# A new order for the opening of a hybrid diffusion backbone: modulation loads first, norm sums and evacuations earlier, small S5 work later

## The chip, the cores and the metric

The kernel runs on one core of a Trainium2 chip. The core has a matrix engine (TensorE, here PE, with its weight loads listed apart as PEld), a vector engine (VectorE, DVE), a scalar engine with function tables (ScalarE, ACT), a general engine (GpSimd, POOL) and a queue for loads and stores (SyncE, SP). The metric is the time of one execution on the device in microseconds, lower is better, given as a median of several runs.

## The reference

The model is a backbone of two layers over 1024 latent tokens with 256 context tokens ahead of them (1280 columns in all), 1024 channels. Both layers begin with an adaptive norm, whose shift, scale and gate come from the conditioning:

```python
def rmsnorm(x, g):
    y = xf * lax.rsqrt(jnp.mean(xf * xf, axis=-1, keepdims=True) + NORM_EPS)
def modulation(cond, w, b):
    return jnp.split(jax.nn.silu(cond) @ w + b, 3, axis=-1)
...
n_lat = rmsnorm(x, norm_g[l]) * (1.0 + sc_l[:, None]) + sh_l[:, None]
n_ctx = rmsnorm(ctx_s, norm_g[l]) * (1.0 + sc_c) + sh_c
```

Layer 0 multiplies the normed tokens with `ev_w_in` (1024 x 3072) and feeds two branches. One is a bidirectional gated recurrence (RG-LRU) behind a short convolution over time. The other is a bidirectional S5 recurrence, whose complex coefficients need sines and cosines of angles:

```python
mag = jnp.exp(lam_re * dt)
ab_re = mag * jnp.cos(lam_im * dt)
ab_im = mag * jnp.sin(lam_im * dt)
f_re = (nr * lam_re + ab_im * lam_im) / den
f_im = (ab_im * lam_re - nr * lam_im) / den
bb_re = f_re[..., None] * b_re - f_im[..., None] * b_im
```

Layer 1 is latent attention with 8 heads; a last norm follows. Everything is float32.

## The kernel before

The channels lie on the partitions and the 1280 tokens in the columns, so the input is eight tiles `xT` of 128 x 1280. A product of float32 precision is made of three passes on PE: each operand is split into a coarse part (`hi`, a cast on ACT) and the rest (`lo`, a difference on DVE), and `mm3` (L209 to L211) adds hi x hi, hi x lo and lo x hi. `split` (L182, L184) does that for weights.

All that the change touches is in `start` (L542), in helpers that it calls, and in the S5 preparation. `start` stands in a `manual_schedule` block: the instructions of each engine run in the order in which the code writes them down, and an engine that waits holds up all that is written behind it on that engine. Loads are issued in written order on SP, of which 8 are in flight; one load waits for the buffer that it overwrites. `big` is a pool of 11 slots and `far` one of 16, each slot 128 x 1280; `mw` tiles (modulation weights) have 6 buffers, `wraw` one.

The opening runs through these stages:

- **Constants and loads.** `load_const` loads small constants, `set_const` makes others, among them `cs` (the SiLU of the conditioning, L245) and `gneg` (the negated gains). `s5_turns` (L359) is a generator that works out the powers of the S5 coefficients: its first piece ends with two sines on ACT (L387, L388), the second multiplies them into powers on DVE and stores them to DRAM as `s5pow` (L390 to L397), the third has 13 small operations on 128 x 32 (L400 to L413) that give the factors `s5f`.
- **Modulation.** `mod_load` loads four `mw` tiles for one unit of 4 channel blocks; `mod_steps` multiplies them (8 matmuls, L277), copies the bank to `row` on DVE (L279), turns it by four small products (L283) and adds the bias on DVE (L287). `norm_scale` (L296) makes the scale. A unit is named (part, half): parts 0, 1, 2 are shift, scale, gate.
- **The first pair.** `pair` (L572) is a generator of ten steps that multiplies two blocks of weights with the eight channel blocks: step i does block i of the first weights (banks "mm") and block i - 2 of the second (banks "g"). `next(run)` writes one step down. The steps use x times the scale, which `x_parts` makes without waiting for the norm: split on ACT (L589) and DVE (L590), a square on ACT (L593), and a running sum `acc` on DVE (L595). Between steps stand the second scale unit (1,1) and the shift units (0,0) and (0,1).
- **The norm.** `sum_of` (L704) sums `acc` over channels on PE with a matrix of ones, in three blocks of columns of 512, 512 and 256. `neg_rstd` (L302 to L309) makes the reciprocal root of each block, with logarithm, exponential and square on ACT and two passes on DVE. `chunks` (L620) copies the finished banks away; for the second block of weights it multiplies by the norm at once, for the first the norm comes later. `shparts` are casts of the shift, two columns of which go into each `xhi` and `xlo` (L723).
- **The second and third pair**, with `normed` and `n_parts` (the normed blocks and their split), `shift_of`, `bias_of` and `put` (the bias of the first two outputs, and their store), and the gate units.
- **Angle pieces and the heads' evacuation.** Beside the third pair, `s5_phases` (L440) makes four pieces: three DVE passes over 128 x 1280 (from L447), then an absolute value and three sines on ACT (L451 to L454). `s5_small` reads the stored powers back and makes the S5 input factors. `conv_in` (L862, L863) empties a finished bank of a recurrence head: a copy and a scaled copy per block of columns on ACT; `conv_tap` (L870) adds the other three taps of the convolution on DVE, and `conv_parts` splits the result. After that the S5 weights begin (`s5_weights`, first at L480). The first SiLU evacuation of the next product on ACT is at L1093.

## Time and profile before

| | |
|---|---|
| median of 3 runs | 1595.79 us (1595.71 to 1597.96) |
| profiled execution | 1596.53 us, of which 1594.4 us from the first to the last instruction |
| mean granted clock of PE | 0.971 |
| PE, DVE, ACT busy | 94%, 71%, 52% of the span |
| bytes moved by DMA | 207.76 MB |

The profile is of one execution. Engines work side by side; what ends a stretch is the engine on which the others wait last there. Idle time of a row is given in square brackets, with the instruction that ended it. The granted clock is a share of the full 2.4 GHz.

### The profile page before, as it was taken

How to read it: one execution, taken by the hardware profiler on the slowest of the kernel's cores; microseconds unless marked ns; L12 is line 12 of the kernel's file. 1: busy time of each engine (PE TensorE's matmuls, PEld its weight loads, DVE VectorE, ACT ScalarE, POOL GpSimd, SP SyncE). 2: the span in 40 equal slices, each digit the busy share in tenths (PEclk: the TensorE clock that was granted, in tenths of full speed). 3: DMA queues.
4: the chain of work that ended last, by engine and by line, in shares of the span. 5: the costliest groups of instructions: out<-in, count | busy, mean ns of one | idle time of the engine just before them, and what ended most of it. 6: DMA issues, size and time to landing. Idle time of an engine off the chain costs nothing.

```text
span 1594.4 us, 22595 instructions
## 1 busy us (share of the span) xinstructions
PE 1495.9 (94%) x8690; PEld 1287.3 (81%) x8690; DVE 1139.5 (71%) x1858; ACT 826.0 (52%) x1422; POOL 46.5 (3%) x107
## 2 busy tenths in 40 slices
PE   6997889989998997899999999999999999999997
PEld 3675777877777876687787999878999999999887
DVE  6487779899999977622235623558888888889655
ACT  5536676678666694301124423446555565566432
POOL 0002000000000000000000000010000000000000
PEclk8898899999999998899999999999999999999999
DMA  9164544536554657555442231352111120122253
GB/s 352 68 212 160 165 143 140 178 125 193 146 153 139 180 176 248 187 178 185 157 177 93 67 87 53 121 186 73 31 50 41 63 58 17 41 93 87 92 180 119
DMA packets 96154, 207.76 MB, mean 130 GB/s; under 512 B 9904, under 2 KB 42416, under 8 KB 96048
## 3 DMA queue, kind: packets, MB, share of 16 engines
q1 hardware_dynamic: 86528, 166.65, 32.0%
q0 software_dynamic: 9520, 39.69, 7.4%
q8 instruction: 68, 1.11, 0.3%
q14 instruction: 38, 0.31, 0.1%
HBM read 143.03 MB, written 63.28 MB: 129 GB/s over the span
## 4 chain that ended last, share of the span: by engine, by line
PE 34%; issue 26%; DVE 12%; DMA 3%; ACT 1%; POOL 1%; SPq 0%; DVEq 0%; POOLq 0%; ACTq 0%
PE pv L1578 7%; PE pt L1565 4%; PE S L209 2%; PE S L210 2%; PE S L211 2%; PE S L1517 2%; PE S L1514 2%; PE S L1516 2%; PE S L1513 2%; PE S L1515 2%; DVE H L1018 1%; DVE u L870 1%; PE pt L210 1%; PE pt L211 1%; PE pt L209 1%
## 5 line engine op out<-in xcount | busy, mean ns | idle before, releaser
L182 ACT CAST w_hi<-wraw 128x1024 fp32r<-128x1024 f32 (+3 forms) x73 | 63.3, 867 | 188.1 <-PE mm L210 132.0
L209 PE MATMUL mm<-n0hi,w_hi 128*128 128x512 f32 (+1 forms) x432 | 157.7, 365 | 0.0
L210 PE MATMUL mm<-n0lo,w_hi 128*128 128x512 f32 (+1 forms) x432 | 154.9, 358 | 0.0
L211 PE MATMUL mm<-n0hi,w_lo 128*128 128x512 f32 (+1 forms) x432 | 154.1, 357 | 0.0
L1569 ACT CAST ph<-pt 128x512 fp32r<-128x512 f32 x160 | 90.9, 589 | 83.3 <-PE pt L1565 83.0
L1572 DVE TENSOR_TENSOR pl<-pt,ph 128x512 fp32r<-128x512 f32 x160 | 109.5, 686 | 19.6 <-ACT ph L1569 17.7
L209 PE MATMUL mm<-hi,w_hi 128*128 128x512 f32 (+1 forms) x264 | 101.1, 383 | 12.7 <-ACT w_hi L182 10.4
L209 PE MATMUL mm<-n1hi,w_hi 128*128 128x342 f32 (+2 forms) x336 | 109.6, 329 | 1.7 <-DVE pr L1321 1.7
L210 PE MATMUL mm<-n1lo,w_hi 128*128 128x342 f32 (+2 forms) x336 | 110.7, 329 | 0.0
L211 PE MATMUL mm<-n1hi,w_lo 128*128 128x342 f32 (+2 forms) x336 | 110.2, 328 | 0.0
L1578 PE MATMUL pv<-ph,v 128*128 128x256 f32 x640 | 107.4, 298 | 0.0
L211 PE MATMUL mm<-hi,w_lo 128*128 128x512 f32 (+1 forms) x264 | 99.7, 381 | 4.8 <-DVE w_lo L184 4.8
L210 PE MATMUL mm<-lo,w_hi 128*128 128x512 f32 (+1 forms) x264 | 99.5, 377 | 0.0
L184 DVE TENSOR_TENSOR w_lo<-wraw,w_hi 128x1024 fp32r<-128x1024 f32 (+3 forms) x73 | 72.4, 992 | 30.4 <-ACT w_hi L182 28.6
L209 PEld LDWEIGHTS mm<-n0hi,w_hi 128*128 128x128 f32 x432 | 82.4, 191 | 12.8
L211 PEld LDWEIGHTS mm<-n0hi,w_lo 128*128 128x128 f32 x432 | 81.9, 190 | 13.0
L210 PEld LDWEIGHTS mm<-n0lo,w_hi 128*128 128x128 f32 x432 | 82.1, 190 | 12.3
L1565 PE MATMUL pt<-c_ident,P 128*128 128x128 f32 x640 | 90.9, 272 | 0.6 <-DVE kl L1495 0.6
L1550 ACT ACTIVATE P<-S,sm 128x512 f32<-128x512 f32 x128 | 86.6, 688 | 0.0
L1578 PEld LDWEIGHTS pv<-ph,v 128*128 128x128 f32 x640 | 84.2, 190 | 0.2
L1565 PEld LDWEIGHTS pt<-c_ident,P 128*128 128x128 f32 x640 | 75.7, 141 | 10.5 <-DVE kl L1495 0.8
L1542 DVE TENSOR_REDUCE sm<-S 128x1 f32<-128x512 f32 x128 | 82.1, 681 | 0.7 <-PE S L1517 0.6
(420 smaller groups left out, 4031.0 us busy)
## 6 DMA issues: line engine op xcount, KB each, us to landing
mw<-in_mod_w SPq DMA_DIRECT2D x48, 512.0 KB
wraw<-in_w_in SPq DMA_DIRECT2D x24, 512.0 KB
mixdr<-r POOLq DMA_DIRECT2D x14, 640.0 KB, 5.8
s5wt<-s5scr SPq DMA_DIRECT2D x16, 512.0 KB
ph<-phdr SPq DMA_DIRECT2D x16, 480.0 KB
wraw<-in_mla_in SPq DMA_DIRECT2D x14, 512.0 KB
wraw<-in_w_out SPq DMA_DIRECT2D x16, 384.0 KB
xT<-in_xT SPq DMA_DIRECT2D x8, 640.0 KB
```

The source lines that it names most:

```text
L182: nc.scalar.copy(hi, raw)
L184: nc.vector.tensor_sub(lo, raw, hi.bitcast(F32))
L209: mm(out, w[0], x[0], start=start, stop=False)
L210: mm(out, w[0], x[1], start=False, stop=False)
L211: mm(out, w[1], x[0], start=False, stop=stop)
L1513: mm(d, q[0][:, qs], k[0][:, ks], start=True, stop=False)
L1542: nc.vector.reduce_max(x.sm[e][:, n:n + 1], x.S[e][n], axis=mybir.AxisListType.X)
L1550: nc.scalar.activation(x.P[e][:, s:s + z], x.S[e][n], AF.Exp, bias=sm[:, 4:5], scale=SCALE, accum_out=sm[:, 5 + n:6 + n])
L1565: nc.tensor.transpose(pt[:, i, e], x.P[e][:, key:key + 128], self.ident)
L1569: nc.scalar.copy(x.hi[t], x.pt[t])
L1572: nc.vector.tensor_sub(x.lo[t], x.pt[t], x.hi[t].bitcast(F32))
L1578: mm(x.pv, v[:, 128 * (h % 2):128 * (h % 2) + 128], p, start=x.left == 30, stop=x.left == 1)
```

## The change

It changes the order of the opening and moves some operations from one engine to another; what is computed stays the same.

- The conditioning is loaded first, then the S5 constants, then the first four `mw` tiles; `sel`, `mod_b` and `gains` come behind these. `gneg` moves behind the first piece of `s5_turns`.
- In `s5_turns` the square and the step 1 - 2x go from DVE to ACT (one Square and one Copy with scale and bias over 128 x 608). The two remaining products and the store are written down later, behind `x_parts(5)` and a further step of the pair. The 13 small operations go to `s5_small`, where they read the powers that were loaded back.
- The shift unit (0,0) is written ahead of `x_parts(6)`, with all its steps before the next step of the pair; the unit (0,1) and the sums of the norm stand ahead of step 7 of the pair, where they stood behind it. The third sum takes a bank "mm", and its norm block stands ahead of the casts of the shift.
- Beside the third pair the first four steps write the first two angle pieces; the third and fourth stand each between `conv_in` and the end of `conv_tap` of one head. `s5_small` is written at step 4 instead of step 1.

```diff
@@ set_const
-        nc.vector.tensor_scalar(self.gneg, self.gains[:, 0:29], -1.0, None, ALU.mult)
@@ s5_turns
...
+        nc.vector.tensor_copy(self.s5_u8, v[:, :, 18])
+        nc.vector.tensor_copy(self.s5_rho, w[:, :, 18])
         nc.scalar.activation(hs, v, AF.Sin, scale=ONE_PI)
         nc.scalar.activation(sn, v, AF.Sin, scale=TWO_PI)
+        nc.scalar.activation(hs, hs, AF.Square)
+        nc.scalar.activation(hs, hs, AF.Copy, bias=1.0, scale=-2.0)
         yield
-        nc.vector.tensor_copy(self.s5_u8, v[:, :, 18])
-        nc.vector.tensor_copy(self.s5_rho, w[:, :, 18])
-        tt(hs, hs, hs, ALU.mult)
-        ts(hs, hs, -2.0, 1.0, ALU.mult, ALU.add)
         tt(hs, hs, w, ALU.mult)
         tt(sn, sn, w, ALU.mult)
         self.s5pow = self.dram.tile([2, 128, 32 * NP], F32, name="s5pow")
         for i, p in enumerate((hs, sn)):
             nc.gpsimd.dma_start(self.s5pow[i], p.rearrange("p g k -> p (g k)"))
-        yield
-        ts(nr, hs[:, :, 17], -1.0, None, ALU.add)
-        ai = sn[:, :, 17]
...
+    def s5_small(self):
...
+        nc.vector.tensor_scalar(nr, Pre[:, :, 17], -1.0, None, ALU.add)
+        ai = Pim[:, :, 17]
         tt(den, LR, LR, ALU.mult)
...
@@ start
-            self.load_const("s5p", "kpow", "cT", "sel", "mod_b", "gains")
+            self.load_const("cT", "s5p", "kpow")
+            m = [self.mod_load(unit(1, 0), mw)]
+            self.load_const("sel", "mod_b", "gains")
             self.set_const()
             turns = self.s5_turns()
             next(turns)
-            m = [self.mod_load(unit(1, 0), mw)]
+            nc.vector.tensor_scalar(self.gneg, self.gains[:, 0:29], -1.0, None, ALU.mult)
...
             x_parts(2)
-            next(turns)
             x_parts(3)
-            next(turns, None)
             steps = self.mod_steps(unit(1, 1), m[1], self.row)
...
             x_parts(5)
             next(run)
+            next(turns, None)
             w2 = [self.split(r, mp, "wx", 2, [128, 8, 128])]
             r = raw(19)
+            steps = self.mod_steps(unit(0, 0), m[2], self.row)
+            next(steps)
             x_parts(6)
+            next(steps, None)
             x_parts(7)
-            steps = self.mod_steps(unit(0, 0), m[2], self.row)
             next(run)
+            next(run)
+            steps = self.mod_steps(unit(0, 1), m[3], self.row)
             next(steps)
-            next(run)
             next(steps, None)
...
+            sum_of(1, "s5", 2)
+            sum_of(2, "s5", 2)
+            self.neg_rstd(sums, rs, 1024)
             ps = next(run)
-            steps = self.mod_steps(unit(0, 1), m[3], self.row)
-            next(steps)
-            sum_of(1)
-            sum_of(2)
             o = [chunks(ps[0], nc.scalar.copy)]
-            self.neg_rstd(sums, rs, 1024)
+            sum_of(0, "mm", 3)
+            self.neg_rstd(sums[2:], rs, 1024)
             next(run)
-            sum_of(0)
-            next(steps, None)
...
-            self.neg_rstd(sums[2:], rs, 1024)
             ps = next(run)
...
             for i in range(10):
                 ps = next(run)
-                if i == 1:
+                if i < 4:
+                    next(phases)
+                if i == 4:
                     small = self.s5_small()
-                if i < 8:
-                    next(phases)
...
                         self.conv_in(h, p, b)
+                    next(phases)
                     for k in range(3):
                         self.conv_tap(h, k)
+                    next(phases)
```

**First place: DVE around the copy of the second scale unit.** The numbers behind the names count tiles. `row` is the copied modulation row, `s5a` the tile of the small S5 operations, `mod` the modulation. Before, DVE has in a row:

```order
L595 TENSOR_TENSOR acc_28_215<-acc_28_215,sq_291 128x1280
L400 TENSOR_SCALAR s5a_121<-s5half_128 128x32
L402 TENSOR_TENSOR s5a_121<-c_s5p 128x32
...
L409 TENSOR_TENSOR s5f<-s5a_121 128x32
...
L413 TENSOR_TENSOR s5f<-s5a_121 128x32
L279 COPY row_316<-s_49_307 128x512
L287 TENSOR_TENSOR mod_116<-s_54_339,c_mod_b 128x4 x2
```

Now DVE has:

```order
L594 TENSOR_TENSOR acc_28_218<-acc_28_218,sq_285 128x1280
L278 COPY row_297<-s_49_288 128x512
L286 TENSOR_TENSOR mod_123<-s_54_320,c_mod_b 128x4 x2
L295 SCALAR_TENSOR_TENSOR mod_123<-mod_123,gneg 128x4 x2
...
L594 TENSOR_TENSOR acc_28_218<-acc_28_218,sq_370 128x1280
L391 TENSOR_TENSOR s5half_134<-s5half_134,s5w_132 128x608
L392 TENSOR_TENSOR s5sin_133<-s5sin_133,s5w_132 128x608
L184 TENSOR_TENSOR wx_lo_398<-wraw_230,wx_hi_396 128x1024
L278 COPY row_411<-s_67_402 128x512
```

The small S5 operations are gone from between the sum `acc` and the row copy; the two S5 products and the split `wx_lo` stand between a later sum and the row copy of the next unit.

**Second place: ACT at the norm.** `chunks` is the copy of the first finished banks, `rs` the norm. Before, ACT has:

```order
L620 COPY chunks_522<-mm_237 128x8x32
L620 COPY chunks_522<-mm_238 128x8x64
L620 COPY chunks_522<-mm_239 128x8x64
L302 ACT_TABLE_LOAD
L302 ACTIVATE rs_76_488<-s_79_518,eps 128x512
L302 ACTIVATE rs_76_488<-s_80_520,eps 128x512
L306 ACT_TABLE_LOAD
L306 ACTIVATE rs_76_488<-rs_76_488 128x512
L307 ACTIVATE row_528<-rs_76_488 128x512
```

Now ACT has:

```order
L301 ACT_TABLE_LOAD
L301 ACTIVATE rs_79_492<-s_80_493,eps 128x512
L301 ACTIVATE rs_79_492<-s_81_495,eps 128x512
L305 ACT_TABLE_LOAD
L305 ACTIVATE rs_79_492<-rs_79_492 128x512
L306 ACTIVATE row_499<-rs_79_492 128x512
...
L619 COPY chunks_527<-mm_240 128x8x32
L619 COPY chunks_527<-mm_241 128x8x64
L619 COPY chunks_527<-mm_242 128x8x64
L301 ACT_TABLE_LOAD
L301 ACTIVATE rs_79_492<-mm_531,eps 128x256
```

The three copies of `chunks` stood ahead of the logarithms and stand now between the first two norm blocks and the third.

**Third place: ACT at the end of the third pair.** `cosine`, `negsin` and `phase` are the tiles of an angle piece, `wh` the coarse part of the next weights, `xa` and `u` the two copies of a head, `row_1283` and `row_1311` the SiLU evacuations of the product that follows. Before, ACT has:

```order
L451 ACTIVATE cosine_1153<-phase_1152 128x1280
...
L454 ACTIVATE cosine_1153<-cosine_1153,half_pi 128x1280
L775 CAST wh_1183<-wraw_843 128x1024
L862 COPY xa_1187<-mm_976 128x256
L863 ACTIVATE u_1188<-mm_976,c_lru 128x256
...
L862 COPY xa_1219<-g_1042 128x256
...
L1093 ACT_TABLE_LOAD
L1093 ACTIVATE row_1283<-mm_1258 128x256
```

Now ACT has:

```order
L453 ACTIVATE cosine_1019<-cosine_1019,half_pi 128x1280
L775 CAST wh_1157<-wraw_829 128x1024
L864 COPY xa_1161<-mm_962 128x256
...
L1095 ACT_TABLE_LOAD
L1095 ACTIVATE row_1283<-mm_1258 128x256
L450 ACTIVATE cosine_1170<-phase_1169 128x1280
...
L453 ACTIVATE cosine_1170<-cosine_1170,half_pi 128x1280
L864 COPY xa_1206<-g_1006 128x256
...
L1095 ACTIVATE row_1311<-mm_1286 128x512
L450 ACTIVATE cosine_1215<-phase_1214 128x1280
```

The fourth angle piece stood ahead of the weight cast and of both heads; now the second piece stands there, and the third and fourth stand behind the copies of the first and the second head, each with a SiLU evacuation ahead of it.

## Rows read from the trace of the kernel before

**Rows 1.** The page, first part: busy time, share of span, instructions.

```profile
PE 1495.9 (94%) x8690; PEld 1287.3 (81%) x8690; DVE 1139.5 (71%) x1858; ACT 826.0 (52%) x1422; POOL 46.5 (3%) x107
```

**Rows 2.** Waits of PE, 0 to 185 us: total, times, longest.

```profile
PE mm L209 <- ACT u L863: 11.2, 1, 11.2
...
PE s L283 <- DVE row L279: 6.6, 3, 4.2
```

**Rows 3.** Windows: length, PE, PEld, DVE, ACT, POOL, PEclk, DMA share, GB/s.

```profile
34.60:42.00 7.40, 7.34 (x25) 6.38 (x26) 4.64 (x10) 5.30 (x7) 0.00 (x0) 0.54 1.05 391
...
103.00:107.00 4.00, 4.00 (x14) 3.35 (x14) 4.00 (x8) 1.05 (x1) 0.00 (x0) 0.57 0.36 145
```

**Rows 4.** Timeline of the first loads and products: start, busy, engine, instruction, [idle before].

```profile
3.56 1.97 SPq L261 DMA_DIRECT2D mw<-in_mod_w  x4
...
11.87 0.69 ACT L388 ACTIVATE s5sin<-s5v 128x608 f32<-128x608 f32 x1
...
14.86 1.55 ACT L589 ACTIVATE xhi<-xT,mod 128x256 fp32r<-128x256 f32 x2 [1.09 <-DVE mod L296]
...
25.70 1.05 PE L277 MATMUL s<-mw,cs 128*32 128x512 f32 x4 [0.29 <-DMA mw<-in_mod_w]
```

**Rows 5.** Timeline of DVE, 31 to 46 us.

```profile
31.60 0.18 DVE L400 TENSOR_SCALAR s5a<-s5half 128x32 f32<-128x32 f32 x1
...
33.92 0.68 DVE L279 COPY row<-s 128x512 f32<-128x512 f32 x1
...
36.23 0.23 DVE L287 TENSOR_TENSOR mod<-s,c_mod_b 128x4 f32<-128x4 f32 x2 [1.63 <-PE s L283]
...
43.88 1.22 DVE L184 TENSOR_TENSOR wx_lo<-wraw,wx_hi 128x1024 fp32r<-128x1024 f32 x1
```

**Rows 6.** Timeline of PE, 42 to 64 us.

```profile
42.28 0.28 PE L209 MATMUL mm<-xhi,w_hi 128*128 128x256 f32 x1
...
49.42 1.92 PE L277 MATMUL s<-mw,cs 128*32 128x512 f32 x16
...
61.22 2.03 PE L704 MATMUL s<-acc,ones 128*128 128x512 f32 x4
```

**Rows 7.** Timeline of ACT and DVE at the norm, 57 to 78 us.

```profile
57.05 1.28 ACT L620 COPY chunks<-mm 128x512 f32<-128x512 f32 x2 [0.33 <-PE mm L211]
...
62.39 0.69 ACT L302 ACTIVATE rs<-s,eps 128x512 f32<-128x512 f32 x1 [2.76 <-PE s L704]
...
68.13 0.63 ACT L307 ACTIVATE row<-rs 128x512 f32<-128x512 f32 x1 [1.02 <-DVE rs L309]
...
73.65 1.28 ACT L302 ACT_TABLE_LOAD   x1
...
77.63 0.42 DVE L308 SCALAR_TENSOR_TENSOR row<-s,row 128x256 f32<-128x256 f32 x1 [5.53 <-ACT row L307]
```

**Rows 8.** Timeline of PE, start of the second pair and a gate unit.

```profile
74.61 0.42 PE L209 MATMUL mm<-xhi,wx_hi 128*128 128x258 f32 x1
...
101.90 1.05 PE L283 MATMUL s<-c_sel,row 128*128 128x2 f32 x8 [1.60 <-DVE row L279]
```

**Rows 9.** Timeline of ACT at the angle pieces, 137 to 161 us.

```profile
137.39 1.28 ACT L451 ACTIVATE cosine<-phase 128x1280 f32<-128x1280 f32 x1 [8.88 <-DVE s5bb L427]
...
145.18 1.27 ACT L451 ACTIVATE cosine<-phase 128x1280 f32<-128x1280 f32 x1 [1.37 <-DVE phase L449]
...
159.83 1.03 ACT L775 CAST wh<-wraw 128x1024 fp32r<-128x1024 f32 x1
```

**Rows 10.** Timeline of DVE, 133 to 181 us.

```profile
133.49 1.49 DVE L447 TENSOR_TENSOR phase<-s5u,c_tau 128x1280 f32<-128x1280 f32 x1
...
163.94 9.23 DVE L870 SCALAR_TENSOR_TENSOR u<-xa,c_lru,u 128x1022 f32<-128x1022 f32 x11 [1.43 <-ACT u L863]
...
180.11 0.28 DVE L480 COPY pad<-s5bb 64x256 f32<-64x256 f32 x1
```

**Rows 11.** DMA issues, 0 to 60 us: queue, count, KB each, us to landing.

```profile
s5pow<-s5sin POOLq DMA_DIRECT2D x1, 304.0 KB, 7.1
```

More of the change, by code (lines that the diff above doesn't have):

```diff
@@ L365, in s5_turns @@
         NP = 19
-        sm = self.far([128, 9, 32], name="s5a")
-        dt, lr, th, n_, u, den, nr, x1, x2 = (sm[:, i] for i in range(9))
-        self.s5_rho, self.s5_u8, self.s5_f = (c.tile([128, *z], F32, name=n)
-                                              for n, z in (("s5rho", (32,)), ("s5u8", (32,)), ("s5f", (2, 32))))
+        sm = self.far([128, 5, 32], name="s5a")
+        dt, lr, th, n_, u = (sm[:, i] for i in range(5))
+        self.s5_rho, self.s5_u8 = (c.tile([128, 32], F32, name=n) for n in ("s5rho", "s5u8"))
         v, w, sn, hs = (self.far([128, 32, NP], name=n) for n in ("s5v", "s5w", "s5sin", "s5half"))
@@ L398, in s5_turns @@
             nc.gpsimd.dma_start(self.s5pow[i], p.rearrange("p g k -> p (g k)"))
-        yield
-        ts(nr, hs[:, :, 17], -1.0, None, ALU.add)
-        ai = sn[:, :, 17]
+    def s5_small(self):
+        nc, t, sp = self.nc, self.t, self.sp
+        tt = nc.vector.tensor_tensor
+        bc = lambda a, k: a.unsqueeze(2).to_broadcast([128, 32, k])
+        Pre, Pim = (sp.tile([128, 32, 19], F32, name=n) for n in ("s5pre", "s5pim"))
+        for i, p in enumerate((Pre, Pim)):
+            nc.sync.dma_start(p.rearrange("p g k -> p (g k)"), self.s5pow[i])
+        sm = sp.tile([128, 6, 32], F32, name="s5small")
+        den, nr, fr, fi, x1, x2 = (sm[:, i] for i in range(6))
+        LR, LI = self.s5p[:, 0], self.s5p[:, 1]
+        nc.vector.tensor_scalar(nr, Pre[:, :, 17], -1.0, None, ALU.add)
+        ai = Pim[:, :, 17]
         tt(den, LR, LR, ALU.mult)
@@ L412, in s5_turns @@
         tt(x1, x1, x2, ALU.subtract)
-        tt(self.s5_f[:, 1], x1, den, ALU.mult)
-    def s5_small(self):
-        nc, t, sp = self.nc, self.t, self.sp
-        tt = nc.vector.tensor_tensor
-        bc = lambda a, k: a.unsqueeze(2).to_broadcast([128, 32, k])
-        Pre, Pim = (sp.tile([128, 32, 19], F32, name=n) for n in ("s5pre", "s5pim"))
-        for i, p in enumerate((Pre, Pim)):
-            nc.sync.dma_start(p.rearrange("p g k -> p (g k)"), self.s5pow[i])
-        fr, fi = self.s5_f[:, 0], self.s5_f[:, 1]
+        tt(fi, x1, den, ALU.mult)
         ccp = sp.tile([128, 2, 32, 16], F32, name="s5c")
```

6 lines of the change are left out of this document (3 added, 3 removed).

## The prediction

> **What bounds the kernel now.** I read the page first: TensorE (PE) is busy for 94% of the span [rows 1], so a stretch in which PE stands still is what an edit of order can win. The diff touches only the opening, the first 185 us. After it the instructions of every engine stand in the same order as before, so I ask one question: by how much earlier does the work after the opening begin? Next I read what PE waits for in 0 to 185 us [rows 2]. The longest wait is 11.2 us for ScalarE's (ACT's) `u`. The next is 6.6 us for VectorE's (DVE's) copy of the modulation row, 4.2 us of it at one place. Third, I read the clock that PE was granted [rows 3]: 0.54 in the 7.4 us after the 4.2 us wait, 0.57 in the 4.0 us that follow a wait of only 1.6 us. Those are mixtures of the levels 1.2 and 2.4 GHz, nearly all 1.2. So here a wait costs its own length and then some more in slow matmuls.
>
> I now carry the shift, new time minus old time of the same work, through the opening.
>
> **The loads.** The four `mw` loads are issued from 3.56 us [rows 4]. In the new order three small loads (`sel`, `mod_b`, `gains`) go behind them, which at about 0.45 us per issue lets the stream begin 1.4 us earlier. The first products are held by ACT instead: it gets two more passes over 608 elements (Square and Copy, which leave DVE). Nothing shows these two; the nearest row, a sine of that shape, takes 0.69 us [rows 4], so ACT is about 1.3 us longer busy. Before the first `xhi` it stood idle 1.09 us [rows 4], waiting for the modulation, so this cover and the earlier start swallow it: the first product moves by 0.9 to 1.1 us. PE then meets the second set of `mw` loads, which it already waits for at 25.70 [rows 4] and which move with the stream. Shift there: between 0 (the small loads come late, and `gneg`, now in front of the first row copy, holds DVE) and -1.4; I take **-1.2**, near the stream, since the waiting row is a load.
>
> **The S5 pieces out of DVE's way.** Before, DVE did the wide pieces ahead of the second of these two parts and the small ones from 31.60 to 33.92 [rows 5], and only then the row copy, for which PE stood 4.2 us. After, the copy stands right behind the third `acc`. DVE is there at about 28.5 us and PE comes to its small products at 29.3, so the wait is gone: -4.2. The stretch 34.6 to 42.0 at 0.54 [rows 3] holds 7.4 x 0.54 = 4.0 us of full-speed work, so without the fall of the clock -3.4. Sum at 42.0: **-8.8**; PE would stand there at 33.2 us.
>
> **A new wait.** What was moved comes back further down. The third modulation unit (`mod_steps` of unit (0,0)) is now asked for after two more pairs of products less than before, and its row copy stands on DVE behind four parts and sums, the two S5 products and the split `wx_lo`. From the second modulation on DVE (36.23 before, 30.35 now: 1.2 + 4.2 and 0.5 for slow small products) to `wx_lo` it takes 43.88 - 36.23 = 7.65 us [rows 5]. Add two S5 products at 0.69 (as wide as the sine [rows 4]), `wx_lo` itself 1.22 and the copy 0.68 [rows 5]: the copy ends at 41.3. PE needs 3.57 us for a pair of steps (42.28 to 49.42 holds two) and 1.92 for the unit [rows 6], so it is there at 39.0: a wait of **2.4 us** that did not exist. It is longer than the wait of 1.6 us after which the clock fell, so I add what 4.0 us at 0.57 lose, 1.7 us [rows 3]. PE runs on at 41.4. It then does the small products 0.9, two pairs 7.1 plus 1.7, the unit of (0,1) 1.9, the round over DVE for its row 0.9, the small products 0.8, and reaches the norm sums at 54.7. They stood at 61.22 [rows 6]. Shift **-6.5**.
>
> The part x7 now waits for the store of the S5 powers, since its tiles take their place. The store is issued at 39.2 and takes 7.1 us [rows 11], to 46.3; two passes later, at 49.3, `acc` is whole, 5 us before the sums want it. Hidden, at 0; without that cover each further microsecond of the store would be one of the sums.
>
> **The norm.** ACT's Ln follows the sums by 1.17 us (62.39 against 61.22 [rows 6, 7]), so now at 55.9. From there to the end of the second Square 68.13 + 0.63 - 62.39 = 6.4 us. Then stand the three copies of the heads' bank, which before were done while ACT waited: 1.28 for two and about 0.35 [rows 7], together 1.6, now on the path. The last norm block takes 77.63 - 73.65 = 4.0 to DVE. DVE's two passes, the two casts of the shift and the first two copies take 1.6. The second pair starts at 55.9 + 6.4 + 1.6 + 4.0 + 1.6 = 69.5; it stood at 74.61 [rows 8]. Shift **-5.1**. PE itself is done with the first pair near 68 to 69, a clock fall at the third wait (for the copy that frees the `mm` bank) included, so ACT decides.
>
> **The second and third pair.** The first products of the pair ran slow before; -0.6. At 101.90 PE waited 1.6 us for a row copy [rows 8]. DVE is now 9 us earlier and PE under 6; by the chain of shift bias, `put`, weight split and row copy the copy ends about 1 us before PE wants it. So -1.6, and -1.7 for the slow stretch behind it [rows 3]. Shift **-9.0** at the end of the third pair; the short waits at 124 us hang on PE's own work and move along.
>
> **The angle pieces.** Before, ACT did all four S5 angle pieces ahead of the heads' evacuation (`conv_in`), from 137.39 to 159.83 [rows 9], and PE stood 11.2 us. After, two stand ahead of it. With -9.0 the first DVE piece starts at 124.5 (133.49 [rows 10]) and ACT at 128.4. A first piece with its table takes 6.3, a further one (159.83 - 145.18)/3 = 4.9, the weight cast 1.0: `conv_in` starts at 140.6, the moment PE ends its third pair. So the 11.2 us are gone, and most of the slow stretch after it. But the rest is late next. DVE's line is: split 1.2, piece 3.8, six taps 6 x 9.23/11 = 5.0, piece 3.8 [rows 10], to 154.4. ACT then has a piece 4.9, a row copy 0.5 and the cast of `u` 1.2, to 161.0; DVE two differences and a split 4.05, to **165.1**, where its S5 weights begin. They began at 180.11 [rows 10]. `s5_small` gets 13 small operations, 33.92 - 31.60 = 2.3 us [rows 5]; they lie beside ACT's second piece, at 0. All queues keep their order from there. Shift **-15.0**.
>
> **Sum.** The profiled execution took 1596.53 us (span 1594.4, and 2.1 around it); 1596.53 - 15.0 = 1581.5. The median is 0.74 lower: **1580.7**.
>
> **Rivals.**
> A, *the wait at 101.90 stays*: my margin is 1 us. Then +1.6 + 1.7: 1584.0. A chance of 0.12. For: DVE is dense there. Against: it gains 4 us on PE.
> B, *the clock forgives*: no fall after the 2.4 us wait, or the norm chain runs shorter; -1.7 to -4: 1577 to 1579. 0.14.
> C, *table switches*: the row copies (SiLU) now alternate with sines on ACT. If each change loaded a table there would be four more loads at 1.28 us [rows 7], all in the chain that ends at 165.1: +5.1, 1585.8. Against: the new order shows one load, ahead of the first row copy. 0.04. The Trainium skill, "ScalarE: Activation LUTs", section "Rules for kernel authors", speaks against this interleaving: do all of one table set before switching, at some 2.7 us a switch, which would make it 1591.5. The profile has 1.28 us for a load, and no run here shows a switch at 2.7.
> D, *given back*: a later stage is paced by loads that do not move, and the time stays 1595 to 1596. For: 208 MB in all. Against: loads wait for buffers that come free earlier. 0.03.
> E, *slower, the clock stays down*: the place is the second pair, some 40 us of PE work at full clock, entered after three waits in a row (39, 53, 60 us). Each microsecond of that work done at 1.2 GHz costs one more. With 15.0 won, the kernel is slower by over 0.2% once 18 us of it run so; with half of it the time is 1600.7. Against: slow stretches lasted 4 to 7.4 us [rows 3]. 0.03.
>
> **How the numbers follow.** The forecast proper, within 2 us of 1580.7, has 0.64, A 0.12, B 0.14, C 0.04, D 0.03, E 0.03. The range takes in A, B and C with the bounds of the loads (+1.2): 1575 to 1588, and leaves about 0.1 out. A measurement can tell about 0.2%, 3.2 us, from no change. Faster by more: 0.64 + 0.12 + 0.14 + 0.04 = 0.94; within: 0.03; slower: 0.03.
>
> **What will show it.** Right: PE has no wait before the second set of small products, a new one of about 2.4 us near 39 us, sums near 54.7, the second pair near 69.5, `conv_in` near 140.6 without a PE wait of 11 us, S5 weights near 165. Wrong: a wait over 4 us at 39 us, the second pair later than 72, a table load between sine and row copy, or a stage after 185 us whose length changes by more than 2 us.

## The result, and the profile after

The changed kernel takes 1579.9 us (median of 4 runs, 1579.71 to 1580.32), beside 1596.88 us for the kernel before in the same comparison. The ratio is 0.9898 with a 95% interval of 0.9883 to 0.9913: faster by 1.0%. The forecast was 1580.7. The profiled execution took 1579.79 us, its span is 1577.7.

The first part of the page of the changed kernel (busy time, share of the span, instructions) answers to [rows 1]:

```profile
PE 1486.9 (94%) x8690; PEld 1277.5 (81%) x8690; DVE 1138.1 (72%) x1856; ACT 828.3 (52%) x1424; POOL 46.8 (3%) x107
```

The shares have hardly moved. PE is busy for 9.0 us less (1495.9 - 1486.9) with the same number of instructions, so in these two executions about that much of the 16.7 us of span is matmuls that ran at the higher clock, and the rest is idle time of PE that is gone.

What PE waits for in the first 170 us of the changed kernel (in total, times, longest), beside [rows 2]:

```profile
PE s L276 <- DMA mw<-in_mod_w: 7.2, 4, 6.4
PE g L209 <- ACT hi L1196: 4.9, 1, 4.9
PE s L282 <- DVE row L278: 2.4, 3, 0.8
...
PE mm L209 <- ACT u L865: 1.2, 1, 1.2
```

The 11.2 us for `u` are 1.2 now. The row copies cost 2.4 us in three waits of at most 0.8, which is one trip from PE to DVE and back; no copy is late any more. New is a wait of 4.9 us for `hi`, the cast of the first head's `u`.

The timeline of PE in the changed kernel at the places that the prediction named (start, busy time, instruction, idle time before):

```profile
25.14 1.05 PE L276 MATMUL s<-mw,cs 128*32 128x512 f32 x4 [0.27 <-DMA mw<-in_mod_w]
...
29.72 0.95 PE L282 MATMUL s<-c_sel,row 128*128 128x2 f32 x8
...
34.13 0.28 PE L209 MATMUL mm<-xhi,w_hi 128*128 128x256 f32 x1
...
37.73 2.22 PE L276 MATMUL s<-mw,cs 128*32 128x512 f32 x12
40.26 1.05 PE L276 MATMUL s<-mw,cs 128*32 128x512 f32 x4 [0.31 <-DMA mw<-in_mod_w]
42.11 1.05 PE L282 MATMUL s<-c_sel,row 128*128 128x2 f32 x8 [0.79 <-DVE row L278]
...
53.88 1.96 PE L707 MATMUL s<-acc,ones 128*128 128x512 f32 x4
...
66.84 0.39 PE L209 MATMUL mm<-xhi,wx_hi 128*128 128x258 f32 x1 [1.92 <-ACT xhi L724]
...
116.25 0.36 PE L209 MATMUL g<-n0hi,w_hi 128*128 128x256 f32 x1 [1.55 <-DVE chunks L621]
```

Beside [rows 4, 6, 8]: the last products of the second modulation unit, which wait for their loads in both kernels, start 0.56 us earlier (25.14 against 25.70), the step of the pair at 34.13 stood at 42.28, the norm sums begin 7.3 us earlier (53.88 against 61.22), the second pair 7.8 us (66.84 against 74.61). At 116.25 stands the first product of the third pair's second block of weights. Before, it was 8.65 us later:

```profile
124.90 0.36 PE L209 MATMUL g<-n0hi,w_hi 128*128 128x256 f32 x1 [1.50 <-DVE chunks L622]
```

ACT and DVE of the changed kernel, the last part of the input and then the evacuation:

```profile
46.57 1.55 ACT L588 ACTIVATE xhi<-xT,mod 128x256 fp32r<-128x256 f32 x2 [6.53 <-issue]
...
139.59 1.03 ACT L775 CAST wh<-wraw 128x1024 fp32r<-128x1024 f32 x1
140.53 0.36 ACT L864 COPY xa<-mm 128x256 f32<-128x256 f32 x1
...
143.69 1.28 ACT L1095 ACT_TABLE_LOAD   x1
144.99 0.39 ACT L1095 ACTIVATE row<-mm 128x256 f32<-128x256 f32 x1
145.71 1.28 ACT L450 ACTIVATE cosine<-phase 128x1280 f32<-128x1280 f32 x1 [0.34 <-DVE phase L448]
...
164.72 0.28 DVE L479 COPY pad<-s5bb 64x256 f32<-64x256 f32 x1
165.01 0.29 DVE L480 COPY pad<-s5bb 64x256 f32<-64x256 f32 x1
```

The first row is the part x7, which waits for the store of the S5 powers, forecast for 46.3. The weight cast stood at 159.83 [rows 9], 20.2 us later. `conv_in` follows at 140.53. The S5 weights start at 164.72 instead of 180.11 [rows 10]: 15.4 us earlier. Set beside each other instruction by instruction, the two traces stay 15.4 to 15.6 us apart on DVE up to 500 us and end 16.7 us apart.

### The profile page after: what moved, and what is told of

It reads as the page before. It is cut to its first block, busy times and chain, and to the rows that moved or that the text cites. A ratio compares the mean times of both kernels' runs of the same rounds, so it can differ in the third digit from the quotient of the medians.

```text
span 1577.7 us, 22599 instructions
## 1 busy us (share of the span) xinstructions
PE 1486.9 (94%) x8690; PEld 1277.5 (81%) x8690; DVE 1138.1 (72%) x1856; ACT 828.3 (52%) x1424; POOL 46.8 (3%) x107
## 4 chain that ended last, share of the span: by engine, by line
PE 35%; issue 26%; DVE 11%; DMA 2%; ACT 1%; POOL 1%; SPq 0%; DVEq 0%; POOLq 0%; ACTq 0%
PE pv L1580 7%; PE pt L1567 4%; PE S L209 2%; PE S L211 2%; PE S L210 2%; PE S L1519 2%; PE S L1518 2%; PE S L1517 2%; PE S L1516 2%; PE S L1515 2%; DVE H L1020 1%; PE mm L211 1%; PE mm L209 1%; PE mm L210 1%; PE pt L210 1%
```

## The experiments

The theory: two gains in series. The opening proper (loads, S5 work out of the way, norm order) brings the third pair forward, and the order at the evacuation brings the rest. What counts of the second is not PE's wait but where the line of DVE and ACT ends, at the S5 weights. Its rivals: PE's waits are themselves the price; one part is swallowed by the other; the clock of PE decides.

Each median below is of 4 to 6 runs. Medians of one kernel differ by up to 2 us between comparisons (the changed kernel had 1579.9 and 1577.84), so a shift of less than 2 us is read from the traces. A trace shows one execution: four executions with the same order up to the second pair (the changed kernel, `after_again`, `opening_only`, `early_hi`) have the norm sums at 53.88, 53.28, 53.29 and 54.91 us and the second pair at 66.84, 66.23, 66.25 and 67.86.

### The two parts alone

`evac_only` is the kernel before with the new loop beside the third pair; `opening_only` is the changed kernel with the old loop:

```diff
 for i in range(10):
     ps = next(run)
-    if i < 4:
-        next(phases)
-    if i == 4:
+    if i == 1:
         small = self.s5_small()
+    if i < 8:
+        next(phases)
 ...
         for b, p in enumerate(ps[h]):
             self.conv_in(h, p, b)
-        next(phases)
         for k in range(3):
             self.conv_tap(h, k)
-        next(phases)
```

That is the edit that makes `opening_only` out of the changed kernel; `evac_only` makes the reverse edit in the kernel before.

> The kernel before with the new order beside the third pair alone (two angle pieces ahead of the heads' evacuation, two between their taps). Theory 1, two gains in series with DVE's line as the limit: the third pair ends where it did, `conv_in` starts near 149.6 us (140.5 of the changed kernel and the 9.0 by which the opening is later), PE's wait of 11.2 us for `u` falls to about 1, and the S5 weights on DVE start near 173.7 us instead of 180.1, because the two late pieces then stand in DVE's and ACT's line. Time 1589.4 us, 6.4 less than before, although PE loses 10 us of waiting. Rival, PE's wait is the price: the whole 11.2 us and the slow stretch behind it are won, 1581 to 1585 us.

> The changed kernel with the old order beside the third pair (four angle pieces ahead of the evacuation, `s5_small` at step 1). Theory 1: the third pair runs 8.7 to 9.0 us earlier than before as in the changed kernel; the 13 small S5 operations, 2.3 us, now stand ahead of the second angle piece, on which ACT waits, so `conv_in` comes 6.5 us earlier than before (near 154 us) and the S5 weights near 173.5. Time 1589.3 us. Theory 1 without a price for the 13 operations: 1587.0. Rival, an earlier opening is swallowed by the angle pieces or by loads: 1594 to 1596 us.

Measured: `evac_only` 1589.66 us, ratio to the kernel before 0.9953 (0.9940 to 0.9966); `opening_only` 1586.63 us, ratio 0.9938 (0.9924 to 0.9952). The product of the two ratios is 0.9891, the whole change has 0.9898. So the parts add, and none swallows the other.

`evac_only`, timeline: ACT's first evacuation and the S5 weights on DVE:

```profile
149.61 0.37 ACT L864 COPY xa<-mm 128x256 f32<-128x256 f32 x1
...
173.79 0.28 DVE L480 COPY pad<-s5bb 64x256 f32<-64x256 f32 x1
```

The longest wait of PE behind its third pair is the one for `hi`, 4.9 us, as in the changed kernel. `conv_in` was expected at 149.6 and the S5 weights at 173.7. PE's wait of 11.2 us is gone from this kernel, yet it won 6.3 us at the S5 weights and 7.7 in time (beside 1597.38 us for the kernel before): the rest came back as the wait of 4.9 us for `hi`. The rival that prices PE's wait falls.

`opening_only`, timeline: ACT's second angle piece and first evacuation, and the S5 weights:

```profile
135.09 1.27 ACT L450 ACTIVATE cosine<-phase 128x1280 f32<-128x1280 f32 x1 [4.02 <-DVE phase L448]
...
150.66 0.36 ACT L862 COPY xa<-mm 128x256 f32<-128x256 f32 x1
...
170.92 0.28 DVE L479 COPY pad<-s5bb 64x256 f32<-64x256 f32 x1
```

Its longest wait of PE:

```profile
PE mm L209 <- ACT u L863: 15.0, 1, 15.0
```

PE has the long wait for `u` again, 15.0 us, since it comes to it earlier. ACT waits 4.02 us for the second angle piece where it waited 1.37 [rows 9]: 2.65 us more. That is the price of the 13 small operations when they stand ahead of a piece, which the prediction put at 2.3 and hid beside ACT in the changed kernel. The time is 2.7 us better than expected. In the profile the first angle piece began at 120.75 us and not at 124.49, with the same order ahead of it, which fits; but that is one execution, the fastest of the five. The section on the clock below takes it up.

### The S5 work in front of the row copy, in three doses

`s5_back` puts the four wide and the 13 small operations back on DVE ahead of the row copy of the second scale unit; `products_small_back` only the two products and the small ones; `products_back` only the two products:

```diff
             x_parts(2)
+            next(turns)
             x_parts(3)
+            next(turns, None)
...
             next(run)
-            next(turns, None)
             w2 = [self.split(r, mp, "wx", 2, [128, 8, 128])]
```

In `products_back` it is one `next(turns, None)` ahead of `x_parts(3)`; `s5_back` and `products_small_back` also take back the pieces of `s5_turns` that the names say.

> The changed kernel with the S5 powers as they were before: all four wide operations on DVE ahead of the part of the third channel block, the 13 small ones ahead of the row copy of the second scale unit. Theory 1: the row copy ends 4.9 us later (33.5 us instead of 28.6), PE waits 3.5 to 4.5 us for it and its clock falls to a mean near 0.54 behind it, 3.4 us more; the wait for the loads of the next unit near 40 us, 1.6 us, is covered. Norm sums near 60 us, time 1585.5 to 1586.5 us. Rival 1, the clock does not fall: 1582 to 1583 us. Rival 2, the loads of the next unit bound this stretch anyway: 1580 to 1581 us.

> The changed kernel with the two S5 products on DVE ahead of the part of the third channel block and the 13 small operations ahead of the row copy, while the square and 1 - 2x stay on ACT. The row copy ends 3.7 us later than in the changed kernel, near 32.3 us, and PE waits 2.6 to 3.0 us for it (4.42 with all four wide operations). Theory 1, a wait of this length too is followed by a slow stretch: 0.54 to 0.6 over the next 7 us, 3 us lost, less 1.6 for the wait for loads near 40 us that is covered: 1584 to 1585 us. Rival, the clock stays at 1.00 behind it: 1581 to 1581.5 us.

> The changed kernel with the two S5 products alone moved back, ahead of the part of the third channel block. The row copy of the unit (1,1) ends 1.4 us later, near 30.0 us, and PE waits 0.4 to 0.8 us for it (2.18 with the 13 small operations too, 4.42 with all). Theory 1: so short a wait brings no slow stretch, and the wait for loads near 40 us covers it: the sums stay within 0.4 us of 53.9 and the time is 1579.0 to 1580.2 us. Rival, any wait before these small products makes the clock fall: 0.5 to 0.9 in the 8 us behind it and 1581 to 1582 us.

Measured: 1583.02 us (1580.41 to 1588.38), 1582.03 and 1580.89. None lies in the range of its theory 1. The first lies at its rival 1, no fall of the clock; its profile, taken from the slowest of the six runs, shows such a fall all the same, and the times alone don't tell the cases apart. So the rest is read from the traces. PE's small products of the unit (with the wait ahead of them) and the norm sums in `s5_back`:

```profile
34.25 1.86 PE L282 MATMUL s<-c_sel,row 128*128 128x2 f32 x8 [4.42 <-DVE row L278]
...
59.24 1.96 PE L708 MATMUL s<-acc,ones 128*128 128x512 f32 x4
```

The stretch behind the wait (the granted clock is the third number from the end):

```profile
34.20:41.60 7.40, 7.35 (x30) 6.53 (x31) 4.31 (x9) 4.98 (x6) 0.00 (x0) 0.66 1.04 385
```

The same of `products_small_back`, timeline and then the stretch behind the wait:

```profile
32.48 1.05 PE L282 MATMUL s<-c_sel,row 128*128 128x2 f32 x8 [2.18 <-DVE row L278]
...
56.67 1.96 PE L708 MATMUL s<-acc,ones 128*128 128x512 f32 x4
```

```profile
32.40:40.00 7.60, 7.52 (x34) 6.51 (x35) 5.32 (x11) 5.96 (x7) 0.00 (x0) 0.78 1.06 391
```

Of `products_back`, with the store of the powers on POOL and the last loads of the next unit:

```profile
25.74 0.68 POOL L395 DMA_DIRECT2D s5pow<-s5half  x1 [25.29 <-DVE s5half L391]
...
29.79 1.05 PE L282 MATMUL s<-c_sel,row 128*128 128x2 f32 x8 [0.19 <-DVE row L278]
...
41.19 1.05 PE L276 MATMUL s<-mw,cs 128*32 128x512 f32 x4 [0.30 <-DMA mw<-in_mod_w]
...
54.87 1.96 PE L707 MATMUL s<-acc,ones 128*128 128x512 f32 x4
```

With all of it the wait is 4.42 us, the clock behind it 0.66, and the sums come 5.4 us later than in the changed kernel (59.24 against 53.88). The wait and 2.5 us of slow matmuls (7.4 x 0.34) make 6.9, of which about 1.6 hide in the wait for loads near 40 us, which this kernel does not have and the changed one does. The prediction charged 4.2 and 3.4 to this place; the clock fell less here than in the kernel before. The dose of 2.18 us costs 2.8 us at the sums, with 0.78: a slow stretch, but half of the expected 3 us. The smallest dose leaves 0.19 us, since the copy was not as late as I took it to be. The sums of `products_back` are 1.0 us later all the same, more than the 0.4 that I allowed, and the place is the next unit: PE meets its last loads at 41.19 instead of 40.26. The store of the S5 powers, twice 304 KB, is issued at 25.74 in this kernel and at 39.46 in the changed one, so it goes through the DMA engines amid the loads of that unit. In the four executions with the changed kernel's opening those last loads are met between 39.61 and 40.26, so 41.19 lies outside. The store fits the delay; it was not tried apart. The prediction had followed this store only at its new place.

### The loads and the norm

`loads_back`:

```diff
-            self.load_const("cT", "s5p", "kpow")
-            m = [self.mod_load(unit(1, 0), mw)]
-            self.load_const("sel", "mod_b", "gains")
+            self.load_const("s5p", "kpow", "cT", "sel", "mod_b", "gains")
...
             nc.vector.tensor_scalar(self.gneg, self.gains[:, 0:29], -1.0, None, ALU.mult)
+            m = [self.mod_load(unit(1, 0), mw)]
```

> The changed kernel with the loads in the old order: all small constants ahead of the first four `mw` tiles. Theory 1, the stream of loads paces the first 25 us and, near 40 us, the unit (0,0): everything from the second set of modulation products on is 1.2 to 1.9 us later (those at 22.0 and 23.8 us, and the norm sums at 53.9 us in the changed kernel): 1581.1 to 1581.8 us. Rival, the engines have slack there and the order of the loads is worth nothing behind 40 us: 1579.5 to 1580.2 us.

Measured: 1581.09 us (1576.85 to 1582.36), which tells neither case from the other. PE in `loads_back`, second modulation unit and norm sums:

```profile
24.02 2.92 PE L276 MATMUL s<-mw,cs 128*32 128x512 f32 x16
...
54.45 1.96 PE L706 MATMUL s<-acc,ones 128*128 128x512 f32 x4
```

The first modulation products start 1.2 us later (7.55 against 6.36). The second unit starts 2.0 us later (24.02 against 22.04), but runs through without a wait for loads to 26.94, where the changed kernel, which waits for them twice, is done at 26.19: 0.75 us. The sums are 0.6 us later, which is less than the spread of executions of one order. So the order of the loads is worth 1.2 us at the start, less than 1 us at the second unit, and what is left of it at the norm these traces do not tell.

`norm_back` puts the unit (0,1) and the sums behind one more step of the pair, the copies of the heads' banks ahead of the logarithms, and the third norm block behind the casts of the shift:

```diff
             next(run)
             next(run)
-            steps = self.mod_steps(unit(0, 1), m[3], self.row)
-            next(steps)
-            next(steps, None)
...
-            sum_of(1, "s5", 2)
-            sum_of(2, "s5", 2)
-            self.neg_rstd(sums, rs, 1024)
             ps = next(run)
+            steps = self.mod_steps(unit(0, 1), m[3], self.row)
+            next(steps)
+            sum_of(1)
+            sum_of(2)
             o = [chunks(ps[0], nc.scalar.copy)]
-            sum_of(0, "mm", 3)
-            self.neg_rstd(sums[2:], rs, 1024)
+            self.neg_rstd(sums, rs, 1024)
             next(run)
+            sum_of(0)
+            next(steps, None)
```

> The changed kernel with the norm as it was: the unit (0,1) and the first two sums behind one more step of the pair, the copies of the heads' banks ahead of the logarithms, the third sum in the shared bank, its norm block behind the casts of the shift. Theory 1: the sums come 1.8 us later (near 55.7) and the chain from them to the second pair takes 13.4 us as before instead of 13.0, so the second pair starts near 69.1 us instead of 66.8 and the time is 1582.2 us. Rival, ACT's copies of the banks, now off the norm's chain, give it back: 1579.9 to 1580.5 us.

Measured: 1583.41 us (1578.11 to 1586.96). PE in `norm_back`, the sums, the second pair, and the small products of the first gate unit:

```profile
55.10 2.04 PE L704 MATMUL s<-acc,ones 128*128 128x512 f32 x4
...
68.48 0.40 PE L209 MATMUL mm<-xhi,wx_hi 128*128 128x258 f32 x1
...
95.75 1.63 PE L282 MATMUL s<-c_sel,row 128*128 128x2 f32 x8 [2.19 <-DVE row L278]
```

The same small products in the changed kernel:

```profile
94.93 0.95 PE L282 MATMUL s<-c_sel,row 128*128 128x2 f32 x8
```

The chain from the sums to the second pair takes 68.48 - 55.10 = 13.4 us, as expected, and 13.0 in the changed kernel. The second pair is 1.6 us later. Beyond that PE waits 2.19 us for the row copy of the gate unit, as it did at 101.90 before [rows 8]; the changed kernel has no wait there, nor have the three other executions with its opening, whatever the clock of their second pair. So the norm's order, not an earlier DVE alone, removed that wait.

### What the new wait near 40 us hangs on

`square_late` puts 1.27 us back on DVE (the square and 1 - 2x) ahead of the row copy of unit (0,0):

```diff
-        nc.scalar.activation(hs, hs, AF.Square)
-        nc.scalar.activation(hs, hs, AF.Copy, bias=1.0, scale=-2.0)
         yield
+        tt(hs, hs, hs, ALU.mult)
+        ts(hs, hs, -2.0, 1.0, ALU.mult, ALU.add)
```

> The changed kernel with the square and 1 - 2x back on DVE, 1.27 us, ahead of the two S5 products where these now stand (before `wx_lo` and the row copy of the unit (0,0)). In the changed kernel that copy was held by PE's products, and these by their loads, with 0.37 us of idle DVE ahead of it. Theory 1, loads and DVE come nearly together there: the copy and the norm sums move 0.9 us, 1580.0 to 1581.0 us by the trace's sums; the four angle operations on ACT at the start stand 1.4 us less, but wait for the modulation, which gives nothing. Rival, DVE has slack of more than 1.3 us there: nothing moves.

Measured: 1581.75 us (1578.09 to 1585.66). PE in `square_late`, the small products of that unit, and then the stretch behind them:

```profile
42.94 1.05 PE L282 MATMUL s<-c_sel,row 128*128 128x2 f32 x8 [2.07 <-DVE row L278]
```

```profile
42.90:50.00 7.10, 7.06 (x40) 6.19 (x41) 4.11 (x7) 2.48 (x3) 0.00 (x0) 1.00 0.61 223
```

They start at 42.94 instead of 42.11, 0.8 us later, and now with a wait of 2.07 us for the row copy. The sums (54.76) follow by 0.9, as theory 1 had it. In the changed kernel DVE stands only 0.37 us idle ahead of that copy, so DVE and the loads come within half a microsecond of each other here. The median, 0.75 us above the range of theory 1, can't tell this.

### Two tries to win more

`early_hi` splits the first head ahead of the second head's taps, since PE waits 4.9 us for it; `lru_early` moves 24 small DVE operations from the front of the first angle piece into a place where DVE stands idle:

```diff
                     next(phases)
+                    if h == 1:
+                        self.conv_parts(0)
                     for k in range(3):
                         self.conv_tap(h, k)
...
-            for h in range(2):
-                self.conv_parts(h)
+            self.conv_parts(1)
```

```diff
                 if i < 7:
                     normed(i + 1)
+                if i == 2:
+                    self.lru_prep()
...
-            self.lru_prep()
...
-        sp = self.big([128, 4, 8, 2], name="lrusp")
+        sp = self.const.tile([128, 4, 8, 2], F32, name="lrusp")
```

> The changed kernel with the split of the first head's `u` (ACT's cast and DVE's difference) ahead of the taps of the second head and ahead of ACT's part of the fourth angle piece; PE waits 4.9 us for that cast in the changed kernel. Theory 1, DVE's line sets the time behind the opening: PE's wait of 4.9 us near 156 us is gone, but DVE loses only its own wait of 1.8 us near 160 us, so the S5 weights start near 163.0 instead of 164.7 and the time is 1578.2 us. Rival, PE's wait is the price: 4.9 us and the slow stretch behind it (0.55 and 0.59 in 160 to 168 us, about 3.4 us), 1571.6 to 1575.0 us.

> The changed kernel with `lru_prep` (two small ACT operations and 24 small DVE operations, 119.8 to 124.5 us on DVE, ahead of the first angle piece) moved to step 2 of the second pair, where DVE stands 3.5 us and ACT 13 us idle (near 80 us); its tile moves to the constants. Theory 1, the line of DVE and ACT from the first angle piece to the S5 weights sets the end: the first piece starts 4.7 us earlier, `conv_in` starts when PE has its first bank ready, 3.9 us earlier, and so do the S5 weights (36.3 us after the first piece of the changed kernel's place, near 160.8): 1575.5 to 1576.5 us. Rival, that line has a cover (PE or the loads come last): 1579 to 1580 us.

Measured: `early_hi` 1577.76 us, `lru_early` 1579.22 us: neither is told from the changed kernel, with 1579.9 and 1577.84. PE in `early_hi`:

```profile
160.91 0.58 PE L209 MATMUL g<-hi,gw_hi 128*128 128x256 f32 x1 [6.17 <-ACT i L918]
```

PE starts the first head's gates at 152.14, but stands then 6.17 us for `i`, the activation that empties their banks, which ACT reaches only behind the angle piece and two more casts. The wait changed its name. From the third pair's product of the second weights to the second copy of the S5 weights (DVE splits the second head behind the first copy here) `early_hi` takes 48.1 us (112.64 to 160.77), the changed kernel 48.8 (116.25 to 165.01). So 0.6 us were won, less than the 1.7 of theory 1 and far from the 4.9 of the rival.

PE and ACT in `lru_early`:

```profile
96.55 1.05 PE L282 MATMUL s<-c_sel,row 128*128 128x2 f32 x8 [3.31 <-DVE row L278]
...
139.57 1.05 ACT L776 CAST wh<-wraw 128x1024 fp32r<-128x1024 f32 x1 [2.56 <-PE mm L210]
```

The stretch of the second and early third pair in `lru_early`:

```profile
84.00:128.00 44.00, 37.66 (x192) 28.32 (x191) 36.79 (x61) 21.47 (x28) 3.71 (x6) 0.92 0.44 152
```

The idle time of DVE was not free: the row copy of the gate unit stood behind the 24 operations, PE waited 3.31 us for it, and its clock was 0.92 in that stretch (1.00 in the changed kernel). In the changed kernel PE has the first banks ready at 135.0, 4.6 us ahead of ACT; here ACT waits 2.56 us for PE until it can cast the next weights, at 139.57, the time of the changed kernel. What the line of DVE and ACT won, PE lost. Not all of PE's loss is the edit's: its second pair began at 68.61, 1.8 us later than in the changed kernel, behind a stretch of 0.76 (42.90 to 50.00) that lies ahead of the edit. The rival that names PE as the cover holds for this place of the 24 operations and this execution; a place with no row copy behind it was not tried.

`best` has both and, besides, the loads of unit (0,0) ahead of the weights:

```diff
-            r = raw(18)
             m.append(self.mod_load(unit(0, 0), mw))
+            r = raw(18)
```

> The changed kernel with `lru_prep` early, the first head's `u` split early, and the loads of the unit (0,0) ahead of those of the weights that are split behind `x_parts(5)`. The first two parts give 3.9 and 0.6 us by theory 1. The third takes the wait for loads at 37.7 to 41.3 us away, but the weights come 5 us later, near 41 us, and the row copy of that unit stands behind their split on DVE: it ends near 44 us instead of 42.1. By that 1577.3 us; if the wait for loads was all that held the unit, 1574.0 us.

Measured: 1579.97 us, above both cases. PE in `best`, then the S5 weights on DVE:

```profile
42.63 1.35 PE L282 MATMUL s<-c_sel,row 128*128 128x2 f32 x8 [2.83 <-DVE row L278]
...
118.45 0.36 PE L209 MATMUL g<-n0hi,w_hi 128*128 128x256 f32 x1 [1.56 <-DVE chunks L621]
...
163.40 0.29 DVE L480 COPY pad<-s5bb 64x256 f32<-64x256 f32 x1
```

The loads no longer hold the unit (16 products in 1.92 us from 37.88), but the row copy behind the late weights does, for 2.83 us, and the sums come at 56.04, 2.2 us later than in the changed kernel. Behind that the first two parts do win: from the third pair to the S5 weights it takes 45.0 us instead of 48.8, 3.8 us beside the 4.5 that they were to give, and PE has no wait for the row copy of the gate unit here, since its second pair ran at 0.72 (66 to 84 us) and came to it later. In the time nothing of this is left.

### The clock of the second pair

`after_again` is the changed kernel once more.

> The changed kernel itself once more, for a second profile. Three executions with the same order of the opening have shown 0.72, 1.00 and 0.91 for the mean granted clock of 66 to 84 us, and the first angle piece on DVE at 124.49, 120.85 and 120.75 us. Theory 1, the slow stretch of the second pair is not set by the order alone: it differs here too, the first angle piece starts anywhere between 120.7 and 124.6 us, and the runs scatter by up to 4 us, 1576.5 to 1581 us. Rival, the order fixes it: 0.72 again, the piece at 124.5 within 0.3 us, the time 1579.7 to 1580.3 us.

Measured: 1577.84 us (1576.78 to 1580.18). The stretch of 66 to 84 us, PE busy all through it once the second pair has begun, in four executions whose instructions stand in the same order up to there. First the changed kernel, then its second profile, then `opening_only`, then `early_hi` (columns: stretch, its length, busy time of PE, PEld, DVE, ACT and POOL, granted clock, DMA share, GB/s):

```profile
66.00:84.00 18.00, 17.16 (x77) 15.03 (x78) 13.84 (x19) 4.19 (x19) 0.00 (x0) 0.72 0.56 204
```

```profile
66.00:84.00 18.00, 17.77 (x89) 15.78 (x90) 15.47 (x20) 5.04 (x21) 0.00 (x0) 0.81 0.56 205
```

```profile
66.00:84.00 18.00, 17.75 (x96) 15.56 (x97) 16.24 (x20) 6.62 (x23) 0.54 (x1) 0.91 0.56 205
```

```profile
66.00:84.00 18.00, 16.14 (x96) 14.24 (x97) 17.00 (x23) 6.68 (x25) 0.09 (x1) 1.00 0.57 205
```

A clock of 0.72 over 18 us takes 5.0 us of full-speed work away, 0.81 takes 3.4, 0.91 takes 1.6. The first angle piece on DVE follows it: 124.49, 122.37, 120.75 and 120.85 us. The 1.00 of `early_hi` is no gain of its own: its slow stretch stood earlier, behind the wait at 41.56 that is 0.79 us long there as in the other three, which ran at 1.00 behind it. So its pair began 1.0 us later than that of the changed kernel:

```profile
42.00:54.00 12.00, 11.16 (x59) 7.98 (x58) 6.42 (x8) 4.00 (x4) 0.00 (x0) 0.86 0.41 150
```

So the order of the program does not fix which stretch runs at 1.2 GHz; the same waits ahead of it gave four clocks, and `opening_only` and `early_hi` ran on the same chip. What fixes it stays open. The Trainium skill, "TensorE: Matmul & The Clock Gate", Part 1, section "What's actually happening", says of the start of a kernel that the number of slow matmuls differs from run to run; these rows show a like spread in the middle of this one. The rival, an order that fixes the clock, falls.

## Why the prediction was right, point by point

- **The S5 pieces out of DVE's way** (shift of -8.8 at 42.0 us): right. The same products stand at 34.13 instead of 42.28, -8.15. Of that -0.56 is there at the second set of loads, so the place itself gave 7.6 us, as much as the 4.2 of waiting and 3.4 of slow matmuls that I had; what is missing is the term of the loads. `s5_back` gave the wait (4.42) and a slow stretch back.
- **The loads**: oversized. -1.2 was taken at the second set; the products that waited for it at 25.70 wait for it at 25.14, -0.6. The stream began earlier (first products at 6.36 instead of 7.48), but did not keep that lead. What is left of it at the norm sums, `loads_back` does not show.
- **The new wait near 39 us**: wrong in cause, nearly right in effect. I had DVE's row copy 2.4 us late. It was the loads of that unit that came late: its 16 products took 37.73 to 41.3 instead of 1.92 us, and the row copy then cost 0.8. DVE itself was about where I had it: free for the copy at 41.0, so that it would have ended near 41.6 (forecast 41.3); the loads were a second limit, 0.4 us later, that I did not have, and `square_late` shows DVE as the limit. PE went on at 42.11, where I had 41.4. The slow stretch of 1.7 us that I added did not come in this execution: the clock was 1.00 there. So the sums stand at 53.88 and not 54.7. In `early_hi` it came (0.86 over 12 us, 1.7 us), and the sums stand at 54.91.
- **The store of the S5 powers** was hidden as forecast: x7 begins at 46.57 (forecast 46.3), `acc` is whole at 50.8, 3 us ahead of the sums.
- **The norm**: the term was oversized. I had 14.8 us from the sums to the second pair, it took 13.0. The 6.4 us that I carried over from ACT's rows held 1.02 us of waiting for `rs` [rows 7], which the new order does not have: ACT goes from 55.02 to the end of the second square with a gap of 0.17 us only (5.3 us). The copies of the banks took 1.3 instead of 1.6, and DVE's tail 1.3 instead of 1.6. The second pair came at 66.84, not 69.5.
- **The second pair**: wrong, and it took back what the norm gave. I expected 3.9 us to be won between its start and the end of the third pair (-5.1 to -9.0); 0.9 were up to the third pair (-7.8 to -8.65), and 1.2 up to the first angle piece, which began at 124.49. The wait at 101.90 is gone as forecast, with its slow stretch, but 66 to 84 us ran at 0.72. I had seen slow stretches only behind waits and had charged them there; rival E named this place, with a larger loss. `after_again` and `opening_only` show that this is the profiled execution's share, and not the order's: in the three other executions of this opening the first angle piece began at 122.37, 120.75 and 120.85. That the profile hit my 124.5 is luck.
- **The angle pieces**: right. `conv_in` at 140.53 (forecast 140.6), S5 weights at 164.72 (165.1), PE's wait 1.2 instead of 11.2. `evac_only` shows the same with the old opening.
- **Rivals.** A (the wait at 101.90 stays) did not come true, though `norm_back` brings that wait back. B (the clock forgives, or the norm runs shorter) came true in both parts in the profiled execution and was paid back in the second pair; the second comparison, at 1577.84, lies in its 1577 to 1579. C (table switches): one load at 143.69 ahead of the first row copy, and none between the row copies and the sines after it, so the 5.1 us were not paid. Nor were the 2.7 us that the Trainium skill, "ScalarE: Activation LUTs", section "Rules for kernel authors", budgets for every switch to a different table set: no load marks a switch here. D fell: the shift of 15.4 us is kept to the end. E fell as a whole.
- **Behind 185 us** the shift grew by 1.3 us, which the forecast did not have. It is within the 2 us that I allowed, and within what executions of one kernel differ by: the second profile of the changed kernel is 2.3 us ahead of the first at 300 us and 0.6 us behind it at the end.

So the sum was right to 0.8 us because two errors nearly cancelled: 2.7 us up to the second pair (0.84 ahead of the sums, 1.84 in the norm) and 3.0 us in the second pair. The base helped too. The forecast takes 15.1 us from 1595.79; beside the kernel before in the same comparison the change won 17.0 us, and 18.9 in the second one.

## What to carry to other kernels

Where one engine is nearly full and others feed it, look for the small operations that stand ahead of a copy or an evacuation for which it waits, and move them behind: here a new order, with two operations moved to another engine, won 17 us. Price it by the line of the engine that comes last behind the place, not by the wait that goes: taking away 11.2 us of PE's waiting won 6 to 8 us, because the moved pieces came back on DVE and ACT. Idle time of an engine is only free if nothing that is waited for stands behind it in its queue. And profile a kernel more than once before a few microseconds are read from one trace.

## What the runs showed of the hardware that was not expected

- One order of instructions gave granted clocks of 0.72, 0.81, 0.91 and 1.00 in the same 18 us, worth up to 5.0 us. A single profile of this kernel is no better than that.
- A wait of 2.07 us (`square_late`) was followed by a clock of 1.00, one of 2.18 us (`products_small_back`) by 0.78. A wait of 0.79 us was followed by 1.00 in three executions and by 0.86 in `early_hi` (42 to 54 us). The length of a wait alone did not tell whether the clock falls.
- SiLU and sine stood alternately on ACT from 143.69 to 159 us in the changed kernel with a single table load of 1.28 us.
